# Running states of a recurrence carried as two chains of two head pairs, with operands stored chunk by chunk

## The chip, the cores and the metric

The kernel runs on one core of a Trainium2 chip. The metric is device time in microseconds (us). The engines are TensorE (PE; PEld is its weight load), VectorE (DVE), ScalarE (ACT), GpSimd (POOL) and the queue engine SyncE (SP), which issues nearly all DMAs here in program order.

## The reference, cut to what matters

The reference is two transformer blocks over 1,024 tokens of 1,024 features. The first block normalises x, multiplies by `w_in`, and feeds two branches: latent attention (MLA, eight heads) and a recurrence (RWKV, eight heads of 64 channels, in both directions of time).

```python
h = rms_norm(x, norm_mix_g[l])
z = h @ w_in[l]
o_mla = mla_branch(z_mla, ...)
o_rwkv = rwkv_branch(z_rwkv, ...)
gates = jax.nn.sigmoid(z_gate + gate_b[l])
mixed = gates[:, :, 0] * (o_mla @ w_br_mla[l]) + gates[:, :, 1] * (o_rwkv @ w_br_rwkv[l])
x = x + mixed @ w_out[l]
```

The rest (a hierarchical mixture of experts, then a block with windowed attention, a gated linear recurrence and expert-choice mixtures) doesn't touch the change. In the RWKV branch each head carries a 64 x 64 state over time. The kernel works in chunks of 64 tokens: all that needs no state is prepared for every chunk, and then the state is carried over 16 chunks, in each direction.

## The kernel before, in words

Tokens are T = 1024, chunks CH = 64, so NCH = 16. A *head pair* puts two heads on 128 partitions; there are four pairs, and each has two directions d.

`phase_a` computes 37 column tiles of z one after the other (`z_tile`: 48 products of 128x512 each) and calls `after(m)` behind each. In `after`, tiles 5, 8, 11 and 14 complete a pair's inputs. `pair(j)` then runs `prep` for the four combinations of half g and direction d, and behind the first of them `inverse(j - 1)` and `rwkv_chain` of pair j - 1. At tile 16 come pair 3, `inverse(3)`, `finish(0, 0)`, the release of preparation's pools (`own.close()`), the chain of pair 3 in pools opened after that (`ch3` and `pc3`), and `finish` of pairs 1 to 3. `mla` comes last in the program, and `branch_out` behind it.

The tile framework places the instructions of each engine by a simulation of its own: what is issued earlier in the program has priority, and what is ready fills the gaps. So tiles of z and MLA's work, which come late in the program, stand between the steps of the recurrence on PE, VectorE and ScalarE. Each engine then works through its fixed order.

`prep` (line 601 on) writes nine parts of 64 columns per chunk to scratch memory `P.rw[p]`, of shape [8, 128, 2, 1152]: two chunks next to each other, [chunk pair, partition, direction, part and chunk]. `put` (L489) stores a tile of eight chunks; `flip` (L525 to L535) transposes a tile and stores it in two DMAs. `inverse` solves a triangular system for each chunk of a pair by a long row of small VectorE instructions (L653, L655), joins the blocks by products (L671, L676), and stores X^T of four units (direction, half), written at L679.

`rwkv_chain` (L717 on) holds one pair in both directions. Per chunk it makes four groups of 64x64x64 products at L732, each into the one PSUM tile `pc` and each evicted before the next: p1 (L739, L740), U (the same lines), the new state S (L773, with the decayed old state SW that POOL makes at L755) and y (L777). VectorE takes partitions 0 to 63 of p1 and U, ScalarE the others. Every second chunk one load of 1,152 KB brings the operands of two chunks (L745), and y of two chunks is stored by two DMAs (L780). The tiles SW, p1, U and S have two buffers.

`finish(p, g)` (L682 on) sums y of both directions, normalises it per head (first product at L688), adds a bonus and a gate and stores half of the pair's output (L2006). It needs all chunks of its pair.

`branch_out` (L983 on) multiplies both branches by their output weights (tiles br).

Of the kernel before, what the change touches and what calls it, by code (L numbers as in the profile page):

```python
# [7 lines left out]
F32 = mybir.dt.float32  # L8
# [19 lines left out]
# ---------------------------------------------------------------- host layout  # L28

def _cols(w, idx):  # L30
    """[K, M] -> [len(idx)//128, 128, (K//128)*128]: tile, k-partition, (k-block, column)."""
    K = w.shape[0]
    t = w[:, idx].reshape(K // 128, 128, len(idx) // 128, 128)
    return np.ascontiguousarray(t.transpose(2, 1, 0, 3).reshape(len(idx) // 128, 128, K))


def _fvec(v):
    """[n*128] -> [128, n]: feature on the partition."""
# [3 lines left out]
def _chunks(w):  # L42
    """[..., K, N] -> [..., N/512 * K/512, 128, 2048]: chunks of 4 k-blocks by 512 columns, k fastest."""
# [7 lines left out]
def _constants():  # L51
    """Constants of the branches, and those of the whole program."""
# [138 lines left out]
# ---------------------------------------------------------------- device program  # L191

class Prog:
# [3 lines left out]
    def consts(self, pool, temp):  # L197
        """pool: for the whole program; temp: for the branches."""
# [17 lines left out]
    def keep(self, keep, dram):  # L216
        """Scratch memory, and the small tiles that several phases use."""
        nc = self.nc
        self.kp = keep
        self.yd = [dram.tile([128, T], F32, name=f"yd{j}") for j in range(8)]  # L220
# [3 lines left out]
        self.rw = [dram.tile([8, 128, 2, 1152], F32, name=f"rw{p}") for p in range(4)]  # L224
# [30 lines left out]
    def slots(self, table, n, base):  # L255
        """What marks the rows in table [128, 8, n, 6]: the row of its block plus base, the block and zero."""
# [5 lines left out]
    def thirds(self, table, x):  # L262
        """x in three bfloat16 parts that add up to it exactly, to table[..., 3:6]; x is overwritten."""
# [7 lines left out]
    def iota8(self, pool):  # L271
        """The slots (from 1), each eight times."""
# [4 lines left out]
    def onehot(self, out, iota8, pm):  # L277
        """out [128, 128, 8]: 1 at the slot pm (from 1) of each row and row block, 0 elsewhere."""
        return self.nc.vector.tensor_tensor(out, iota8, pm[:, None, :].to_broadcast([128, 128, 8]), op=OP.is_equal)

    def mm3(self, ps, lh, ll, rh, rl, first, last):
        """One K block of a float32 product from operands split into float32r parts."""
# [5 lines left out]
    def order(self, later, first):  # L288
        """`later` is issued behind `first` on their engine: one accumulation at a time in a bank."""
# [3 lines left out]
    def rsqrt(self, pool, out, v, n):  # L293
        """out = v ** -0.5 by Newton steps; out, v: [128, n]."""
# [16 lines left out]
    def rsqrt1(self, pool, out, v):  # L311
        """The same for one column where ScalarE has its square root at hand."""
# [9 lines left out]
def s1(P, hpool, wpool, psum):  # L322
    """Reads x, normalises it and leaves its transpose, split, in hT (hi, lo)."""
# [1711 lines left out]
```

## Time and profile before

| what | value |
|---|---|
| runs of the kernel before | 4,285.96, 4,307.15, 4,308.72 us; median 4,307.15 |
| span of the profiled execution | 4,303.5 us |
| PE busy | 3,854.9 us (90%) |
| PEld busy | 3,100.3 us (72%) |
| VectorE busy | 2,887.8 us (67%) |
| ScalarE busy | 2,145.3 us (50%) |
| POOL busy | 418.9 us (10%) |
| DMA | 925 MB, mean 215 GB/s |

The profile is of one execution. Busy time is the union of an engine's instructions; a matmul's end is modelled, so a busy PE isn't a PE at its peak. Idle time before an instruction is put down to what ended last. "Issue" is time in which an engine waited for nothing that the profile shows. Times in the rows below are microseconds from the span's start, durations of single instructions nanoseconds where a row says mean ns or min/median/max.

### The profile page before, as it was taken

Reading aid. Unit: us, or ns where it says so; the run is one execution under the profiler, and the core shown is the slowest. Engines: PE = TensorE matmul, PEld = TensorE weight load, DVE = VectorE, ACT = ScalarE, POOL = GpSimd, SP = SyncE. Lnnn points to the kernel's source line nnn. Section 1 sums busy time; section 2 is a strip of 40 time slices with the busy share of each in tenths; the row PEclk is TensorE's granted clock in tenths of the full one; section 3 lists DMA queues with packets and bytes.
Section 4 is the critical chain, followed back from the end, with each engine's and each line's share of the span. In section 5 each row is a group of like instructions: output and inputs, shape, how many; then the busy total and the mean of one; then the engine's idle time right before and its main releaser. Section 6 shows DMA issues by size and latency. Waiting matters only on the chain. (4 is left out here: it accounts for less than half of the span.)

```text
span 4303.5 us, 57981 instructions
## 1 busy us (share of the span) xinstructions
PE 3854.9 (90%) x22154; PEld 3100.3 (72%) x22154; DVE 2887.8 (67%) x4690; ACT 2145.3 (50%) x2829; POOL 418.9 (10%) x328
## 2 busy tenths in 40 slices
PE   7999988898998897999799969999969986999994
PEld 6877766776876676665679857787748875788773
DVE  4556375858557546654446758888876776788887
ACT  4322223333243224555335536777756852677774
POOL 0000000000010003333000001111010000111101
PEclk9999988988899898999899979999979997999997
DMA  3455665453435557997332359999941155899994
GB/s 106 140 169 148 182 196 161 120 153 92 150 107 173 212 193 269 317 304 227 120 132 82 131 205 338 370 376 384 373 158 69 69 202 207 304 359 377 384 373 168
DMA packets 362342, 925.00 MB, mean 215 GB/s; under 512 B 147600, under 2 KB 205712, under 8 KB 290128
## 3 DMA queue, kind: packets, MB, share of 16 engines
q1 hardware_dynamic: 343632, 870.93, 56.4%
q0 software_dynamic: 18432, 50.36, 4.7%
q8 instruction: 175, 2.87, 0.3%
q14 instruction: 103, 0.84, 0.1%
HBM read 770.68 MB, written 167.25 MB: 218 GB/s over the span
## 5 line engine op out<-in xcount | busy, mean ns | idle before, releaser
L253 DVE TENSOR_TENSOR wlo<-wraw,whi 128x2048 fp32r<-128x2048 f32 x498 | 1134.2, 2289 | 307.1 <-ACT whi L253 303.8
L253 ACT ACTIVATE whi<-wraw 128x2048 fp32r<-128x2048 f32 x498 | 955.0, 1919 | 378.3 <-PE g L286 254.0
L285 PE MATMUL g<-wlo,xth 128*128 128x512 f32 x1280 | 510.0, 398 | 6.7 <-DVE wlo L253 6.7
L284 PE MATMUL g<-whi,xth 128*128 128x512 f32 x1280 | 513.7, 402 | 2.3 <-ACT xth L253 1.6
L286 PE MATMUL g<-whi,xtl 128*128 128x512 f32 x1280 | 508.4, 397 | 7.7 <-DVE xtl L253 7.3
L286 PEld LDWEIGHTS g<-whi,xtl 128*128 128x128 f32 x1280 | 243.5, 190 | 63.7 <-DVE xtl L253 12.7
L285 PEld LDWEIGHTS g<-wlo,xth 128*128 128x128 f32 x1280 | 244.0, 191 | 61.4 <-DVE wlo L253 9.1
L284 PEld LDWEIGHTS g<-whi,xth 128*128 128x128 f32 x1280 | 244.4, 191 | 57.3 <-ACT xth L253 3.9
L284 PE MATMUL z<-hT_hi,w_hi 128*128 128x512 f32 x592 | 243.0, 411 | 9.7 <-ACT w_hi L253 6.7
L1635 POOL DMA_INDIRECT e_xg<-xm,e_ix x32 | 75.5, 2359 | 1719.5 <-DVE e_ix L1633 956.6
L285 PE MATMUL z<-hT_lo,w_hi 128*128 128x512 f32 x592 | 242.0, 409 | 0.0
L286 PE MATMUL z<-hT_hi,w_lo 128*128 128x512 f32 x592 | 241.0, 408 | 0.0
L285 PE MATMUL g<-wlo,e_hh 128*128 128x512 f32 x512 | 202.4, 398 | 15.5 <-DVE wlo L253 15.5
L284 PE MATMUL g<-whi,e_hh 128*128 128x512 f32 x512 | 204.3, 400 | 8.2 <-ACT e_hh L253 8.0
L286 PE MATMUL g<-whi,e_hl 128*128 128x512 f32 x512 | 196.5, 391 | 0.2
L904 PE MATMUL po<-V,pts 128*128 128x64 f32 x1024 | 142.5, 285 | 6.3 <-DVE tab L856 4.9
L284 PEld LDWEIGHTS z<-hT_hi,w_hi 128*128 128x128 f32 x592 | 115.2, 195 | 41.5 <-ACT w_hi L253 7.4
L904 PEld LDWEIGHTS po<-V,pts 128*128 128x128 f32 x1024 | 135.4, 204 | 12.1 <-DVE tab L856 5.2
L755 POOL TENSOR_SCALAR SW<-S,wc 128x64 f32<-128x64 f32 x120 | 65.5, 563 | 785.0 <-DVE S L773 701.3
L285 PEld LDWEIGHTS z<-hT_lo,w_hi 128*128 128x128 f32 x592 | 115.0, 194 | 30.4 <-issue 4.5
L286 PEld LDWEIGHTS z<-hT_hi,w_lo 128*128 128x128 f32 x592 | 114.4, 193 | 30.0 <-issue 3.8
L1235 PE MATMUL g<-wraw,m_hT 128*128 128x512 f32 x256 | 120.3, 610 | 13.1 <-ACT m_y L1236 8.1
(531 smaller groups left out, 8308.7 us busy)
## 6 DMA issues: line engine op xcount, KB each, us to landing
wraw<-in_w_gu SPq DMA_DIRECT2D x256, 1024.0 KB
wraw<-in_w_dn SPq DMA_DIRECT2D x128, 1024.0 KB
wraw<-in_w SPq DMA_DIRECT2D x96, 1024.0 KB
rwt<-rw SPq DMA_DIRECT2D x32, 1152.0 KB
w_raw<-in_w_in SPq DMA_DIRECT2D x37, 512.0 KB
rw<-flip SPq DMA_DIRECT2D x96, 128.0 KB
rw<-rAR SPq DMA_DIRECT2D x16, 512.0 KB
gt<-z_out SPq DMA_DIRECT2D x16, 512.0 KB
```

The costliest lines, as they stand in the source:

```text
L253: return self.nc.scalar.activation(hi, src, AF.Copy), self.nc.vector.tensor_sub(lo, src, hi.bitcast(F32))
L284: t.matmul(ps, lh, rh, start=first, stop=False)
L285: t.matmul(ps, lh, rl, start=False, stop=False)
L286: t.matmul(ps, ll, rh, start=False, stop=last)
L755: nc.gpsimd.tensor_scalar(SW[:, d], S[:, d], P.wc[:, c, 4 * d + p:4 * d + p + 1], None, op0=OP.mult)
L904: i = nc.tensor.matmul(po[:, q], pt[:, k], V[:, 4 * q + k, 64 * par:64 * par + 64], start=(k == 0), stop=(k == 3))
L1235: nc.tensor.matmul(ps, ht[:, k], w[:, k, n], start=(k == 0), stop=(k == 1))
L1635: nc.gpsimd.indirect_dma_start(out=xg, out_offset=None, in_=self.x, in_offset=bass.IndirectOffsetOnAxis(ap=ix[:, :1], axis=0))
```

## The change

The running states are carried in two chains of two pairs each (q = 0: pairs 0 and 1; q = 1: pairs 2 and 3). In a chain the four combinations of pair and direction (u = 0 to 3) go through each chunk together: each group at L732 has twice the products, each eviction twice the columns (256). Chain 0 is issued behind `inverse(1)`, chain 1 behind `inverse(3)`, `finish(0, 0)` and `own.close()`, both with the pools `ch` and `pc`. `finish(1)` uses `pc3`.

The scratch memory becomes `P.rw[q]` of shape [16, 128, 2, 2, 576]: [chunk, partition, pair, direction, part], nine parts of 64 columns. Loads are one per chunk; stores write 64 columns (256 bytes) where they wrote 128; a flip is stored by four DMAs instead of two. y goes to `P.yd[q]` chunk by chunk in one DMA. SW, p1 and U have one buffer, S two. SW is one product of POOL with a broadcast instead of two scalings. The other lines of the diff take out comments and texts.

```diff
-        self.yd = [dram.tile([128, T], F32, name=f"yd{j}") for j in range(8)]
+        self.yd = [dram.tile([4, 128, T], F32, name=f"yd{j}") for j in range(2)]
...
-        self.rw = [dram.tile([8, 128, 2, 1152], F32, name=f"rw{p}") for p in range(4)]
+        self.rw = [dram.tile([NCH, 128, 2, 2, 576], F32, name=f"rw{p}") for p in range(2)]
...
     def put(self, p, d, g, m, t):
-        self.P.nc.sync.dma_start(self.P.rw[p][4 * g:4 * g + 4, :, d, 128 * m:128 * m + 128].rearrange("g p t -> p g t"),
-                                 t.rearrange("p (g c) t -> p g (c t)", c=2))
+        self.P.nc.sync.dma_start(self.P.rw[p // 2][NH * g:NH * g + NH, :, p % 2, d, CH * m:CH * m + CH]
+                                 .rearrange("c p t -> p c t"), t)
...
         for c in range(2):
-            o = 128 * m + 64 * c
-            nc.sync.dma_start(P.rw[p][4 * g:4 * g + 4, :, d, o:o + 64].rearrange("g (h t) k -> t (g h) k", h=2),
-                              t[64 * c:64 * c + 64].rearrange("t (x k) -> t x k", k=64))
+            x = t[64 * c:64 * c + 64].rearrange("t (g h k) -> t g h k", h=2, k=64)
+            for h in range(2):
+                nc.sync.dma_start(P.rw[p // 2][NH * g + c:NH * g + NH:2, 64 * h:64 * h + 64, p % 2, d,
+                                               CH * m:CH * m + CH].rearrange("g t k -> t g k"), x[:, :, h])
...
-        wc = P.wc[:, NH * g:NH * g + NH, 4 * d + p:4 * d + p + 1]
+        wc = P.wc[:, NH * g:NH * g + NH, 2 * p + d:2 * p + d + 1]
...
-        nc.sync.dma_start(P.rw[p][4 * g:4 * g + 4, :, d, 0:256].rearrange("g p t -> p g t"),
-                          AR.rearrange("p (g c) t -> p g (c t)", c=2))
+        nc.sync.dma_start(P.rw[p // 2][NH * g:NH * g + NH, :, p % 2, d, 0:128].rearrange("c p t -> p c t"), AR)
...
-        y, y1 = self.load("y0", P.yd[p], g), self.load("y1", P.yd[4 + p], 1 - g)
+        yd = P.yd[p // 2][2 * (p % 2):2 * (p % 2) + 2]
+        y, y1 = self.load("y0", yd[0], g), self.load("y1", yd[1], 1 - g)
...
-def rwkv_chain(P, pool, psum, p):
+def rwkv_chain(P, pool, psum, q):
...
-    U2 = range(2)
+    U4 = range(4)
...
-            for u in U2:
+            for u in U4:
...
     def ev(dst, ps):
-        nc.vector.tensor_copy(dst[0:64], ps[0:64, 0, 0:128].rearrange("p (u t) -> p u t", t=CH))
-        nc.scalar.activation(dst[64:128], ps[64:128, 1, 0:128].rearrange("p (u t) -> p u t", t=CH), AF.Copy)
+        nc.vector.tensor_copy(dst[0:64], ps[0:64, 0, 0:256].rearrange("p (u t) -> p u t", t=CH))
+        nc.scalar.activation(dst[64:128], ps[64:128, 1, 0:256].rearrange("p (u t) -> p u t", t=CH), AF.Copy)
 
     for c in range(NCH):
-        if c % 2 == 0:
-            R = pool.tile([128, 2, 1152], F32, name="rwt", bufs=2)
-            nc.sync.dma_start(R, P.rw[p][c // 2])
-            Y = pool.tile([128, 2, 2, CH], F32, name="Y", bufs=2)
-        o = c % 2
-        A, Rr = (R[:, :, 128 * o + CH * m:128 * o + CH * m + CH] for m in range(2))
-        LA, MB, MK, BT, KT, VT, XT = (R[:, :, 128 * m + CH * o:128 * m + CH * o + CH] for m in range(2, 9))
-        new = lambda name: pool.tile([128, 2, CH], F32, name=name, bufs=2)
+        R = pool.tile([128, 4, 576], F32, name="rwt", bufs=2)
+        nc.sync.dma_start(R, P.rw[q][c].rearrange("p a d t -> p (a d) t"))
+        Y = pool.tile([128, 4, CH], F32, name="Y", bufs=2)
+        A, Rr, LA, MB, MK, BT, KT, VT, XT = (R[:, :, CH * m:CH * m + CH] for m in range(9))
+        new = lambda name, bufs=1: pool.tile([128, 4, CH], F32, name=name, bufs=bufs)
         pst = lambda: psum.tile([128, 2, 512], F32, name="pc", bufs=1)
         if S is not None:
             SW = new("SW")
-            for d in U2:
-                nc.gpsimd.tensor_scalar(SW[:, d], S[:, d], P.wc[:, c, 4 * d + p:4 * d + p + 1], None, op0=OP.mult)
+            nc.gpsimd.tensor_tensor(SW, S, P.wc[:, c, 4 * q:4 * q + 4][:, :, None].to_broadcast([128, 4, CH]),
+                                    op=OP.mult)
...
-            Sn = new("S")
+            Sn = new("S", 2)
             for h in range(2):
-                src = ps[h2[h], h, 0:128].rearrange("p (u t) -> p u t", t=CH)
+                src = ps[h2[h], h, 0:256].rearrange("p (u t) -> p u t", t=CH)
...
-            nc.scalar.activation(Y[h2[h], :, o], ps[h2[h], h, 0:128].rearrange("p (u t) -> p u t", t=CH), AF.Copy)
-        if o:
-            for d in range(2):
-                nc.sync.dma_start(P.yd[4 * d + p][:, CH * (c - 1):CH * (c + 1)], Y[:, d].rearrange("p c t -> p (c t)"))
+            nc.scalar.activation(Y[h2[h]], ps[h2[h], h, 0:256].rearrange("p (u t) -> p u t", t=CH), AF.Copy)
+        nc.sync.dma_start(P.yd[q][:, :, CH * c:CH * c + CH].rearrange("u p t -> p u t"), Y)
...
-                rwkv_chain(P, p("ch3"), pc3, 3)
-                finish(1)
+                rwkv_chain(P, ch, pc, 1)
+                finish(1, pc3)
...
-                        rwkv_chain(P, ch, pc, j - 1)
+                        if j == 2:
+                            rwkv_chain(P, ch, pc, 0)
```

## Rows read from the trace of the kernel before

**Rows 1.** Windows by stage: length, engines' busy, granted clock, DMA share, GB/s.

```profile
590.00:700.00 110.00, 81.96 (x610) 65.18 (x609) 61.53 (x123) 27.21 (x61) 10.43 (x16) 0.71 0.57 168
700.00:1140.00 440.00, 395.13 (x3378) 324.02 (x3379) 300.62 (x741) 154.19 (x384) 29.79 (x56) 0.86 0.48 136
1140.00:1360.00 220.00, 216.90 (x2551) 175.03 (x2549) 142.00 (x406) 94.63 (x262) 22.19 (x49) 1.00 0.36 119
1360.00:1500.00 140.00, 107.65 (x510) 78.77 (x510) 86.08 (x156) 39.51 (x52) 2.01 (x4) 0.84 0.63 220
```

**Rows 2.** The same view for line L732 alone: PE and PEld busy.

```profile
430.00:590.00 160.00, 16.82 (x384) 13.33 (x384) 0.97 0.59 183
590.00:700.00 110.00, 17.46 (x328) 14.26 (x328) 0.71 0.57 168
...
sum 955.00, PE 176.53 PEld 144.49; mean PE 44.13 PEld 36.12
```

**Rows 3.** Groups by line, 430 to 1,390: busy us, mean ns; idle before, releasers.

```profile
L755 POOL TENSOR_SCALAR SW<-S,wc 128x64 f32<-128x64 f32 x120 | 65.5, 563 | 785.0 <-DVE S L773 701.3 <-DVE S L771 83.5
L894 DVE COPY pts<-pt 128x512 f32<-128x512 f32 x64 | 43.9, 686 | 10.9 <-PE pt L889 9.7 <-PE po L904 0.5
L777 ACT ACTIVATE Y<-pc 64x128 f32<-64x128 f32 x128 | 34.5, 269 | 78.4 <-PE pc L732 76.9
L773 DVE TENSOR_TENSOR S<-pc,SW 64x128 f32<-64x128 f32 x112 | 32.2, 288 | 33.8 <-PE pc L732 32.7
L739 DVE COPY p<-pc 64x128 f32<-64x128 f32 x64 | 17.8, 279 | 32.7 <-PE pc L732 32.4
```

**Rows 4.** Waits, 430 to 1,390: engine, line, releaser; us in total, times, longest.

```profile
PEld pc L732 <- issue: 46.6, 107, 2.1
PE pc L732 <- ACT U L740: 10.7, 7, 2.9
PE pc L732 <- DVE S L773: 9.2, 8, 2.0
```

**Rows 5.** Line L773 in two windows: min/median/max ns, first and last start.

```profile
L773 DVE TENSOR_TENSOR S<-pc,SW x28: 272/289/295, 808.2 to 1034.7; 64x128 f32<-64x128 f32 x28
L773 DVE TENSOR_TENSOR S<-pc,SW x28: 274/289/295, 1200.3 to 1276.9; 64x128 f32<-64x128 f32 x28
```

**Rows 6.** Inverse(3)'s outputs (line L679), and chain 0's start on the timeline.

```profile
L679 DVE TENSOR_TENSOR rXT<-pw,xt x4: 424/425/425, 1095.7 to 1131.2; 128x256 f32<-128x256 f32 x4
...
432.89 2.13 SPq L745 DMA_DIRECT2D rwt<-rw  x2
439.35 0.69 PE L732 MATMUL pc<-rwt 64*64 64x64 f32 x8
```

**Rows 7.** Timeline (start us, us) around the stage's end; attention's products; branch_out's products.

```profile
1370.36 1.13 PE L688 MATMUL pc<-y,cstb 128*128 128x512 f32 x2 [0.51 <-DVE yc L713]
1382.56 0.80 SPq L780 DMA_DIRECT2D yd<-Y  x2
1390.99 1.99 PE L688 MATMUL pc<-y,cstb 128*128 128x512 f32 x2
1421.39 1.02 PE L688 MATMUL pc<-y,cstb 128*128 128x512 f32 x2
1456.25 0.32 SPq L2006 DMA_DIRECT2D orw<-yc  x1
...
L904 PE MATMUL po<-V,pts x1024: 217/275/475, 706.9 to 1359.8; 128*128 128x64 f32 x171
...
L284 PE MATMUL br<-oh,whi x128: 387/392/1414, 1392.0 to 1581.5; 128*128 128x512 f32 x128
```

**Rows 8.** DMA from 160 to 1,140 (980 us), and the flips' issues (min/median/max ns).

```profile
DMA packets 204753, 150.57 MB, mean 154 GB/s; under 512 B 125369, under 2 KB 177337, under 8 KB 201867
q1 hardware_dynamic: 204675, 149.53, 52.3%
L534 SPq DMA_DIRECT2D rw<-flip x96: 574/627/1990, 199.7 to 1000.9; - x96
```

## Prediction

> **What bounds the kernel now.** I first cut the span by stage [rows 1]: the change touches only the projection and the two branches, which end near 1,500 us; what lies behind runs on other data and should only shift. In these stages TensorE (PE) is the fullest engine: 217 of 220 us from 1,140 to 1,360, 395 of 440 before that, 82 of 110 from 590 to 700 (at a granted clock of 0.71) and only 108 of 140 from 1,360 to 1,500. VectorE has 301 of 440 us, ScalarE about half of that. So PE is nearly full while latent attention is there to fill it, and it has holes in two places: from 590 to 700, between the projection and attention, and from 1,360, behind attention's last product.
>
> Next I asked what the running states cost. Their products (L732) hold PE for 177 us, of which only 17 and 17 us lie before 590 and 700 [rows 2]. Their 64x128 evictions take 0.27 to 0.29 us each [rows 3]. Then the waits: PE stands still in front of L732 for 10.7 us behind the eviction of U and 9.2 us behind S; its weight loads stand 46.6 us in 107 pieces for no instruction that the trace shows, which is mostly the change from a 128-row to a 64-row product [rows 4]. That is small. The states matter as a chain of latencies: each chunk is four products and four evictions in strict order over one PSUM tile, so the length of a step is what counts. With inverse and preparation beside it a step takes (1034.7 - 808.2) / 13 = 17.4 us; where two of the four chains run side by side (28 adds are 7 joint steps), (1276.9 - 1200.3 - 1.0) / 6 = 12.6 us, the 1.0 being the second chain's lag [rows 5].
>
> Last, who ends the stage. Chain 3 may open its pools only when preparation's memory is released; it stores its last output at 1,382.6. The last pair's finish then begins at 1,391.0 and 1,421.4 and stores its second half at 1,456.3, while the output projection of the branches begins at 1,392 [rows 7]. So latency of states and finish, not PE, ends this stage.
>
> **The change part by part.** *Steps.* 64 steps of one pair become 32 steps of two pairs. Products are the same in number and size, so PE's 177 us stay. Evictions become 64x256. Between 0.279 us at 128 columns and 0.686 us at 512 [rows 3] a straight line gives 0.279 + 128 x 0.407 / 384 = 0.41 us. VectorE: 64 x 4 x 0.28 = 72 us become 32 x 4 x 0.41 = 53; ScalarE about 69 become 50. These 19 us each lie beside PE and are worth nothing by themselves. POOL's 120 products of 64 columns (0.563 us) become 30 of 256 columns; between 0.56 and 4 x 0.563 = 2.25 us each, I take the middle, and either end is hidden, because SW is wanted only three evictions later.
>
> *The last chain.* It no longer waits for the pools behind `own.close()`, only for the first outputs of inverse(3). These come at 1,095.7 to 1,131.2, four of them evenly [rows 6]; chunk 0 needs the first two, 1,107.5. From a load's issue to its first product took 439.35 - 432.89 = 6.5 us [rows 6]; with the store ahead of it I take 8.5, so it starts at 1,116. For 16 joint steps the bounds are 12.6 and 17.4 us [rows 5]. The nearest row is the joint one, which has this very work; four steps still stand beside inverse and the first finish, so 12 x 12.6 + 4 x 17.4 = 221 us: end at 1,337 (1,318 to 1,394). The joint row pays two evictions per hop where one 64x256 will do: 2 x 0.279 - 0.41 = 0.15 us, four hops, 16 steps: 9 us less, 1,328.
>
> *The finish.* Where only pair 3 was left behind the last chain, pairs 2 and 3 are now: four halves. Pair 1 gets a PSUM tile of its own and leaves the tail. The first half began 8.4 us after the last store (1,382.6 to 1,391.0). Successive halves began 20.6 us apart (1,370.4 to 1,391.0) and 30.4 us apart where the output projection ran beside them, and the last half took 34.9 us from there to its store [rows 7]. I take 20.6 twice and the middle, 25.5, once: 1,328 + 8.4 + 66.7 + 34.9 = 1,438, against 1,456.3: 18 us gained (with the ends of the spacing 13 to 23; with the ends of the step 27 gained to 48 lost).
>
> *PE's own sum.* The 34 us of products before 700 [rows 2] move behind it, as the first chain now waits for inverse(1), and 17 of them were done in the thin stretch 590 to 700. Against it: half of the stalls, 19.9 / 2 = 10 us; of the 46.6 us in front of weight loads half would go if each were a change of product size, 23, and none if not: 12; and the projection ends up to 17 us earlier, of which attention, whose start needs VectorE and ScalarE too, can use between 0 and 17: 8. Attention's last product moves from 1,359.8 [rows 7] to 1,360 + 34 - 10 - 12 - 8 = 1,364 (at worst 1,394). Both are ahead of 1,438, so PE doesn't set the end, but only just.
>
> *Layout.* Stores of L, B and K parts, X^T and the masks (64 DMAs) become 256-byte pieces where they were 512, AR's 16 DMAs 512 where they were 1,024, y 256 where it was 512: 32,768 + 8,192 + 8,192 = 49,000 more packets. At most each costs what a mean packet cost: 52.3% of 980 us over 204,753 packets is 2.5 ns of all 16 engines [rows 8], 123 us in 1,200, and the share goes from about 0.5 to 0.6; bytes are the same, so the other end is zero. Nothing in the stage waits for bandwidth at 0.6, so I book nothing; without that cover a store of X^T lands some 1.3 us later, four times on the path. The flips' 96 DMAs (already 256-byte pieces) become 192 of half the size: their issue costs 0.627 us [rows 8], so SP spends 0 to 60 us more in 16 preparations, up to 4 us each. Behind them on SP stand the loads of the next preparation and of the chain. I take it that the store that inverse waits for isn't the one behind them and book nothing, with 4 x 4 = 16 us at the far end. Loads of rwt stay 32 of 1,152 KB, but each now feeds one step and not two.
>
> The Trainium skill (DMA: Bandwidth & Descriptors, Specifications) speaks against this part: below 512 bytes a transfer falls under line rate, since the engine reads, modifies and writes. [...] The trace neither shows nor excludes it for these stores; its flips go to the same memory in 256-byte pieces already.
>
> *Buffers.* SW, p1 and U have one buffer where they had two. Each is overwritten only behind a product that precedes its writer on PE or VectorE anyway, so no wait is added. Sum: 4,303.5 - 18 = 4,285.5 us of span; the median of the runs, 4,307.15, stands 3.65 us above the span, so 4,289.
>
> **Rivals.** (1) *PE alone is the limit, and the tail closes.* If steps run faster than the joint row (VectorE has one eviction per hop and no second chain), the finishes slip under attention, and the output projection starts behind 1,364 and not at 1,392; with part of the 32 us of holes after 1,360 [rows 1] that is 28 to 40 us: about 4,273. For it: PE is idle 32 us there. Against it: joint steps still took 12.6 us with PE full. (2) *The step is late for its data.* One load per step with two buffers leaves one step, 12.6 us, from a buffer's release to its next use, and a load needs 6.5 us plus SP's delay; before, it had two steps. SP issues in order; if it is over 6 us late, each step grows to the 17.4 us row: the end is 1,394 instead of 1,337, 57 us, and so 39 us lost instead of 18 gained: about 4,346. For it: the load sits on a queue with many waiting stores. Against it: among PE's waits in front of L732 the longest are for evictions, none of these for a load [rows 4]. (3) *The moved work binds.* Attention ends at 1,394, the projection of the branches starts after it: 34 us late, less the 18 to 26 that the tail gives: about 4,317. For it: 590 to 700 gets emptier, and its clock of 0.71 would be no better. (4) *The small pieces cost more than booked.* Stores hold each of four preparations up by the 4 us of SP and the 1.3 us of the store: 21 us, about 4,310. For it: all of it lies ahead of the last chain. Against it: bytes are the same. The rule of the Trainium skill's DMA page named above would act here.
>
> **How the numbers follow.** Forecast 0.45 (4,289, own spread 20 either way), rival 1 0.22, rival 2 0.15, rival 3 0.12, rival 4 0.06. Half a per cent, 21.5 us, is about what a measurement of this kernel can tell from no change: below 4,286 is faster, above 4,329 slower. The forecast puts 0.20 below and 0.25 inside; rival 1 goes below, rivals 3 and 4 mostly inside, rival 2 above with some of 3 and 4: 0.42, 0.39, 0.19. The range runs from 4,248 (rival 1 with the forecast's best step) to 4,340.
>
> **What would show it.** Right: the last chain's first load at about 1,112, joint adds 12 to 13 us apart, its last output at 1,320 to 1,345, attention's last product by 1,375 and the last finish stored near 1,440. Adds 17 us apart with PE waiting for rwt show rival 2; attention ending past 1,385 rival 3; a last store of the finish before 1,400 rival 1; X^T of inverse(3) after 1,145 rival 4. The forecast is wrong altogether if the planned order around inverse moves, so that its outputs come tens of microseconds elsewhere.

## The result, and the profile after

The changed kernel took 4,322.75 us (median of 4 runs, 4,319.75 to 4,332.88) against 4,304.61 (4 runs, 4,285.96 to 4,308.72): a ratio of 1.0058, 95% interval [1.0039, 1.0078]. It is slower by 0.6%, where 4,289 was forecast. The profiled execution spans 4,331.1 us, 27.6 more than the kernel before. It is the slowest of the four runs (4,332.88), 10 us above their median, so the times below hold some 10 us that aren't the change's; one trace can't tell where they lie.

First the windows by stage (length, busy time of PE, PEld, VectorE, ScalarE and POOL, granted clock, DMA share, GB/s), which answer to [rows 1]:

```profile
440.00:590.00 150.00, 140.53 (x665) 111.46 (x664) 72.54 (x162) 40.46 (x62) 0.00 (x0) 0.93 0.59 171
590.00:700.00 110.00, 80.79 (x416) 62.88 (x417) 69.62 (x143) 31.30 (x64) 2.71 (x6) 0.70 0.46 121
700.00:1140.00 440.00, 389.70 (x3779) 322.75 (x3777) 307.76 (x703) 151.32 (x347) 16.37 (x25) 0.88 0.53 142
1140.00:1360.00 220.00, 205.48 (x2545) 168.00 (x2546) 129.42 (x332) 80.37 (x193) 8.95 (x13) 0.96 0.44 146
1360.00:1500.00 140.00, 98.51 (x563) 67.56 (x562) 70.12 (x145) 26.79 (x36) 1.23 (x2) 0.69 0.51 178
```

PE has more holes than before in every one of them (from 440 to 590 it was busy all 150 us), and most in the stage that [rows 1] showed nearly full: 14.5 us of 220 free from 1,140 to 1,360, where it was 3. PE became less full while the time grew, so the added time isn't added work of PE. The next view is of the single lines that end the stage: the third pair's inverse (L679), the last chain's adds of S (L772) and stores of y (L777), the finish's first product (L689) and its stores (L2004). Columns are min/median/max ns, then the first and last start; the window is 1,055 to 1,500, where L2004 stores all eight halves and L689 works on pairs 1 to 3, twice per half.

```profile
L679 DVE TENSOR_TENSOR rXT<-pw,xt x4: 425/425/425, 1111.8 to 1143.1; 128x256 f32<-128x256 f32 x4
...
L772 DVE TENSOR_TENSOR S<-pc,SW x28: 405/422/428, 1173.6 to 1381.1; 64x256 f32<-64x256 f32 x28
...
L777 SPq DMA_DIRECT2D yd<-Y x16: 370/371/624, 1156.5 to 1394.8; - x16
...
L2004 SPq DMA_DIRECT2D orw<-yc x8: 319/320/320, 1162.9 to 1487.9; - x8
...
L689 PE MATMUL pc<-y,cstb x12: 590/1059/1221, 1186.6 to 1454.4; 128*128 128x512 f32 x12
```

The inverse's first output comes 16 us later than in [rows 6], its last 12. The chain's steps are (1394.8 - 1156.5) / 15 = 15.9 us apart, neither 12.6 nor 17.4 [rows 5]. The last y is stored 12 us later than before and the last half of the finish at 1,487.9, 31.6 us later [rows 7]. What follows that store is the same: 4,303.5 - 1,456.3 = 2,847 us before, 4,331.1 - 1,487.9 = 2,843 after. So the whole loss of this execution has been made when that store is issued.

The single instructions cost what was expected. Groups from 430 to 1,400 us (busy us, mean ns; idle before):

```profile
L776 ACT ACTIVATE Y<-pc 64x256 f32<-64x256 f32 x64 | 24.2, 377 | 51.9 <-PE pc L734 51.4
L772 DVE TENSOR_TENSOR S<-pc,SW 64x256 f32<-64x256 f32 x56 | 23.6, 421 | 15.6 <-PE pc L734 15.1
L753 POOL TENSOR_TENSOR SW<-S,wc 128x256 f32<-128x256 f32 x30 | 22.2, 741 | 547.3 <-DVE S L772 487.2 <-DVE S L770 60.0
L741 DVE COPY p<-pc 64x256 f32<-64x256 f32 x32 | 13.2, 413 | 15.8 <-PE pc L734 15.5
```

The 64x256 eviction takes 0.41 us, as the straight line through [rows 3] gave. What makes a step long is seen on the timeline of one (start us, us; PE's products and the evictions, weight loads and POOL left out):

```profile
1272.97 0.86 DVE L772 TENSOR_TENSOR S<-pc,SW 64x256 f32<-64x256 f32 x2 [0.21 <-PE pc L734]
...
1274.96 0.68 PE L734 MATMUL pc<-rwt,S 64*64 64x64 f32 x16
...
1275.48 0.63 PE L734 MATMUL pc<-rwt 64*64 64x64 f32 x16
...
1275.94 0.63 PE L734 MATMUL pc<-rwt,U 64*64 64x64 f32 x16
1276.62 0.77 ACT L776 ACTIVATE Y<-pc 64x256 f32<-64x256 f32 x2
...
1277.93 0.68 PE L734 MATMUL pc<-S,rwt 64*64 64x64 f32 x16
...
1278.45 0.63 PE L734 MATMUL pc<-rwt 64*64 64x64 f32 x16
1279.13 0.42 DVE L741 COPY p<-pc 64x256 f32<-64x256 f32 x1
1280.39 0.38 ACT L742 ACTIVATE p<-pc 64x256 f32<-64x256 f32 x1
...
1282.61 0.68 PE L734 MATMUL pc<-p,rwt 64*64 64x64 f32 x16
1283.34 0.42 DVE L741 COPY U<-pc 64x256 f32<-64x256 f32 x1 [0.37 <-PE pc L734]
1283.79 0.38 ACT L742 ACTIVATE U<-pc 64x256 f32<-64x256 f32 x1 [0.15 <-DVE U L741]
...
1286.12 0.68 PE L734 MATMUL pc<-rwt 64*64 64x64 f32 x16
```

Four groups stand one behind the other: y, p1, U, S. None begins before the group ahead of it has been evicted from the one tile `pc`, and after each eviction 0.5 to 2 us pass until PE's order comes back to the chain (1277.39 to 1277.93, 1280.77 to 1282.61, 1284.17 to 1286.12). PE isn't idle in the pauses, it is in attention's products (busy all 100 us from 1,240 to 1,340); but with both pairs in step there is no second chain whose products could stand there.

Two more looks at the same chain. In the stretch in which attention fills PE and no half of the finish stands beside the chain, the steps are (1340.1 - 1244.9) / 6 = 15.9 us, so the finish beside the first steps isn't what makes them long:

```profile
L777 SPq DMA_DIRECT2D yd<-Y x7: 370/371/377, 1244.9 to 1340.1; - x7
```

Behind attention a step took 10.5 us (stores at 1,340.1 and 1,350.6), and then two took 17.4 and 18.0. In the first of these ScalarE stood 6.4 us for a load of attention's output, with the eviction of U behind it in its order; in the second PE had products of the branches' output projection between the groups. Against the step before them these two cost 14 us more.

```profile
1358.53 0.63 ACT L253 ACTIVATE oh<-oraw 128x512 fp32r<-128x512 f32 x1 [6.39 <-DMA oraw<-om]
1359.18 0.38 ACT L742 ACTIVATE U<-pc 64x256 f32<-64x256 f32 x1
```

DMA from 160 to 1,140 us, and then the flips' issues (min/median/max ns), which answer to [rows 8]:

```profile
DMA packets 249181, 145.84 MB, mean 149 GB/s; under 512 B 199248, under 2 KB 222160, under 8 KB 246800
## 3 DMA queue, kind: packets, MB, share of 16 engines
q1 hardware_dynamic: 249104, 144.82, 53.4%
```

```profile
L535 SPq DMA_DIRECT2D rw<-flip x192: 574/615/1922, 201.3 to 1037.5; - x192
```

44,428 more packets raised the share by 1.1 points; those under 512 bytes rose by 73,879, since stores of 512 bytes became pairs of 256. Per byte the engines were held 5% longer (53.4 / 144.82 against 52.3 / 149.53).

### The profile page after: what moved, and what is told of

Read it like the earlier page. It is cut to its first block, busy times and chain, and to the rows that moved or that the text cites. A ratio compares the mean times of both kernels' runs of the same rounds, so it can differ in the third digit from the quotient of the medians.

```text
span 4331.1 us, 57644 instructions
## 1 busy us (share of the span) xinstructions
PE 3845.1 (89%) x22154; PEld 3095.0 (71%) x22154; DVE 2881.3 (67%) x4566; ACT 2129.2 (49%) x2701; POOL 374.0 (9%) x238
## 5 line engine op out<-in xcount | busy, mean ns | idle before, releaser
L284 PE MATMUL z<-hT_hi,w_hi 128*128 128x512 f32 x592 | 243.0, 410 | 10.5 <-ACT w_hi L253 7.9
L880 ACT ACTIVATE p<-S,nm 128x512 f32<-128x512 f32 x128 | 87.4, 685 | 124.3 <-DVE nm L878 111.4
L1232 PE MATMUL g<-wraw,m_hT 128*128 128x512 f32 x256 | 119.5, 606 | 12.6 <-ACT m_y L1233 6.3
```

Source lines behind the costliest of these rows:

```text
L284: t.matmul(ps, lh, rh, start=first, stop=False)
L880: nc.scalar.activation(p, S, AF.Exp, bias=nm, scale=sc, accum_out=rs[:, b, q:q + 1])
L1232: nc.tensor.matmul(ps, ht[:, k], w[:, k, n], start=(k == 0), stop=(k == 1))
```

## The experiments

All ratios are to the kernel before on the same chip, with 95% intervals. Because every kernel spends 2,839 to 2,849 us behind the last store of the finish, the table of four times from the traces tells nearly all of each profiled execution. One execution of each kernel was traced, and the runs of one kernel lie 4 to 35 us apart, so a difference of a few microseconds between two rows says nothing. "X^T" is the first output of the third pair's inverse (pairs counted from 0), "last y" and "last half" are the last stores of the last chain and of the finish.

| kernel | ratio | X^T | last y | last half | span |
|---|---|---|---|---|---|
| before | 1 | 1,095.7 | 1,382.9 | 1,456.3 | 4,303.5 |
| the change | 1.0058 | 1,111.8 | 1,394.8 | 1,487.9 | 4,331.1 |
| e1_layout | 0.9942 | 1,074.0 | 1,371.5 | 1,440.2 | 4,288.6 |
| e3_first_joint | 1.0001 | 1,110.8 | 1,387.3 | 1,452.0 | 4,295.9 |
| e4_last_joint | 0.9983 | 1,070.5 | 1,356.0 | 1,451.0 | 4,294.1 |
| e5_two_psum | 1.0030 | 1,110.7 | 1,349.6 | 1,481.7 | 4,325.2 |
| e6_free_finish | 1.0037 | 1,101.2 | 1,385.4 | 1,471.9 | 4,317.9 |
| e7_flips_four | 0.9972 | 1,073.2 | 1,358.9 | 1,441.6 | 4,282.2 |
| e8_tail_one_pair | 0.9985 | 1,109.2 | 1,397.9 | 1,456.3 | 4,302.0 |
| e9_no_chain0 | 0.9950 | 1,091.0 | 1,359.4 | 1,423.1 | 4,262.4 |
| e10_two_tiles_early | 0.9938 | 1,086.0 | 1,295.4 | 1,433.3 | 4,279.6 |
| e11_two_tiles_pair1_first | 0.9971 | 1,087.4 | 1,364.9 | 1,455.6 | 4,295.4 |
| e12_loads_swapped | 0.9932 | 1,061.8 | 1,356.0 | 1,422.0 | 4,267.8 |
| e13_one_memset | 0.9991 | 1,087.9 | 1,375.6 | 1,448.7 | 4,298.1 |
| e14_after_swapped | 1.0015 | 1,096.3 | 1,371.5 | 1,463.6 | 4,309.6 |
| e15_after_memset | 1.0053 | 1,109.1 | 1,388.7 | 1,481.8 | 4,322.8 |
| e16_layout_swapped | 0.9989 | 1,103.9 | 1,380.2 | 1,461.0 | 4,301.0 |
| e17_two_tiles_swapped | 0.9986 | 1,100.0 | 1,312.3 | 1,453.3 | 4,292.6 |

**The parts alone.** The stores, the first joint chain and the last one can be taken apart: `rwkv_chain1` is the loop of before for one pair, reading the new layout with one load of two chunks; where a kernel also has a joint chain, it has that one's buffers. (The joint chains on the old layout weren't tried.)

e1_layout, the stores alone:

```diff
-                        if j == 2:
-                            rwkv_chain(P, ch, pc, 0)
+                        rwkv_chain1(P, ch, pc, j - 1)
...
-                rwkv_chain(P, ch, pc, 1)
-                finish(1, pc3)
+                rwkv_chain1(P, p("ch3"), pc3, 3)
+                finish(1)
```

> The layout of the change alone: scratch memory chunk by chunk, 64-column stores and four DMAs per flip, but four chains of one pair as before (one load of two chunks). Theory 1, the tail (one long last chain with four finish halves behind it costs the time): within 8 us of the kernel before, inverse(3)'s outputs within 5 us of 1,096 to 1,131. Theory 2, the layout (small stores and the doubled flips delay preparation): 12 to 25 us slower than before, inverse(3)'s outputs at about 1,112 to 1,143 as in the kernel after.

Measured: 4,278.85 us, ratio 0.9942 [0.9918, 0.9966]. The new stores don't slow this kernel; whether they speed it up is taken up again below.

e3_first_joint, the stores and the first joint chain, then pairs 2 and 3 alone:

```diff
+                        if j == 3:
+                            rwkv_chain1(P, ch, pc, 2)
...
-                rwkv_chain(P, ch, pc, 1)
-                finish(1, pc3)
+                rwkv_chain1(P, p("ch3"), pc3, 3)
+                finish(1)
```

> Layout of the change and a joint first chain (pairs 0 and 1), but pairs 2 and 3 as two chains of one pair in the places of before. Theory 1: the tail is that of before, so within 8 us of the kernel before, last state output near 1,385. Theory 2: 12 to 25 us slower than before. If the joint first chain itself cost time, it would be slower than the layout alone.

Measured: 4,299.36 us, ratio 1.0001 [0.9983, 1.0019]. Against e1 the third inverse's outputs come 37 us later, the last y 16 and the last half 12.

e4_last_joint, the stores and the last joint chain:

```diff
-                        if j == 2:
-                            rwkv_chain(P, ch, pc, 0)
+                        if j < 3:
+                            rwkv_chain1(P, ch, pc, j - 1)
```

> The stores of the change, pairs 0 and 1 in chains of one pair as before, pairs 2 and 3 in the joint last chain. Theory A (each part has a price of its own: stores -0.6%, first chain +0.6%, last chain +0.6%): steps of the last chain 15 to 17 us apart, its last y store near 1,385, the last store of the finishes 88 to 93 us behind that, near 1,475; ratio to the kernel before 0.999 to 1.004. Theory B (the joint last chain only costs what the joint first chain makes late): the last chain starts near 1,085 instead of 1,126, the last store of the finishes is at 1,445 or before, ratio 0.995 or less.

```profile
L772 DVE TENSOR_TENSOR S<-pc,SW x28: 405/422/429, 1131.7 to 1334.8; 64x256 f32<-64x256 f32 x28
...
L777 SPq DMA_DIRECT2D yd<-Y x16: 370/371/732, 1115.2 to 1356.0; - x16
```

Measured: 4,291.73 us, ratio 0.9983 [0.9971, 0.9995], between the two theories. The steps are 16.1 us as in the change, and the tail from the last y to the last half is 95.0 us; but the inverse's outputs are back at 1,070.5, so the long steps and the long tail belong to the last joint chain. The late inverse goes with the first one in the kernels so far; how far that holds is taken up again below.

**The tail.** e6_free_finish and e8_tail_one_pair let finishes behind the last chain read the y of pairs that are long done, and leave out their own y (e6 for pairs 2 and 3, e8 for pair 2):

```diff
 e6_free_finish
-        yd = P.yd[p // 2][2 * (p % 2):2 * (p % 2) + 2]
+        yd = P.yd[0][2 * (p % 2):2 * (p % 2) + 2]
 e8_tail_one_pair
+        yd = P.yd[p // 3][2 * (p % 2):2 * (p % 2) + 2]
...
-                finish(2)
-                finish(3, pc3)
+                finish(2, pc3)
+                finish(3)
```

> The kernel after, but the finishes of pairs 2 and 3 read y of pairs 0 and 1, so that they needn't wait for the last chain (y of pairs 2 and 3 isn't used). Theory 1: the four halves go under the last chain; the branches' output starts when attention ends and the stage ends with it: 50 to 90 us below the kernel after, 4,235 to 4,275. Theory 2: preparation's delay stays, 0 to 35 us below the kernel after.

Measured: 4,319.51 us, ratio 1.0037 [1.0018, 1.0056]. The finishes still began at 1,385 to 1,438, although their y had long been there: pair 2 is finished on `pc`, which the chain holds to its end (its first product, at 1,385.4, had waited for the last eviction of y), and pair 3 behind pair 2. This run priced nothing; the next one gave pair 2 the other tile.

> The change, but the finish of pair 2 reads the y of pair 0 and has the PSUM tile of pair 1's finish, so that only pair 3 is finished behind the last chain. Left out: pair 2's own y is not used. If the tail's two added halves are what the joint last chain costs, the last store comes 65 to 75 us behind the last y store (88 to 93 with the change), near 1,465, and the ratio falls from 1.006 to 0.999 to 1.002. If the chain itself is what is late, the last store stays within 8 us of that of the change and the ratio is 1.004 or more.

```profile
L777 SPq DMA_DIRECT2D yd<-Y x16: 370/371/987, 1147.8 to 1397.9; - x16
L2004 SPq DMA_DIRECT2D orw<-yc x8: 319/320/383, 1154.2 to 1456.3; - x8
```

Measured: 4,294.98 us, ratio 0.9985 [0.9970, 1.0000]. The last y came as late as with the change, the last half 58.4 us behind it and not 93 (65 to 75 were expected). The two halves that the change adds behind its last chain are worth 1.0058 - 0.9985 = 0.7%, about the whole loss. That is what they cost, not what made the kernel slower: they were foreseen, and an earlier end of the chain was to pay for them.

**The step.** e5_two_psum gives the y products of the last chain a PSUM tile of their own:

```diff
-        ps = pst()
+        ps = pst(other or psum)
         mm(ps, lambda u: ([(S[:, u], Rr[:, u])] if S is not None else []) + [(VT[:, u], MK[:, u]), (Ut[:, u], MB[:, u])])
...
-                rwkv_chain(P, ch, pc, 1)
+                rwkv_chain(P, ch, pc, 1, pc3)
```

> The kernel after, but in the last chain the group for y has a PSUM tile of its own (that of pc3), so the next chunk's first group needn't wait for y's eviction. Theory 1: the step of the last chain falls from 15.9 us to 12 to 13.5, its last output from 1,395 to about 1,345 to 1,360, and the time 30 to 45 us below the kernel after, about 4,275 to 4,295. Theory 2: the start of the last chain is what counts, so 0 to 10 us below the kernel after.

Measured: 4,319.60 us, ratio 1.0030 [1.0003, 1.0057]. The y stores run from 1,185.8 to 1,349.6, 10.9 us apart, but they begin 29 us later, since `pc3` opens late, and pair 1's finish now waits for the same tile, so six halves stand behind the chain: the step of theory 1, without its time. e10_two_tiles_early removes the late start (on the base of e4, with pair 0's finish issued ahead of the third inverse), and e11_two_tiles_pair1_first also takes pair 1's finish out of the tail:

```diff
 e10_two_tiles_early
-                R.inverse(3)
                 finish(0, 0)
+                R.inverse(3)
                 own.close()
                 R.big, pc3 = p("fin"), p("pc3", space=PS)
-                rwkv_chain(P, ch, pc, 1)
+                rwkv_chain(P, ch, pc, 1, pc3)
                 finish(1, pc3)
 e11_two_tiles_pair1_first
+                finish(1)
                 rwkv_chain(P, ch, pc, 1, pc3)
-                finish(1, pc3)
```

> Pairs 0 and 1 in chains of one pair, the last chain joint, with its y products in a PSUM tile of their own (pc3), which opens sooner because the finish of pair 0 is issued ahead of the third inverse. Theory S (the step is long because all four groups go through one PSUM tile): the last chain's y stores come 11 to 13 us apart from the start (16.1 with one tile), it ends at 1,290 to 1,320 instead of 1,356; six halves of the finish follow, 17 to 19 us apart, and the last store comes at 1,415 to 1,450, ratio 0.992 to 0.998. Theory C (the short steps seen with two tiles came from a start after the inverse and the first finish): steps stay at 15 to 17 us, the end at 1,350 or later, and with six halves behind it the last store near 1,480, ratio over 1.003.

The same lines of this kernel, and a piece of one step:

```profile
L772 DVE TENSOR_TENSOR S<-pc,SW x28: 416/423/428, 1124.4 to 1282.4; 64x256 f32<-64x256 f32 x28
...
L777 SPq DMA_DIRECT2D yd<-Y x16: 359/371/385, 1114.3 to 1295.4; - x16
...
L2071 SPq DMA_DIRECT2D orw<-yc x7: 319/320/457, 1074.7 to 1433.3; - x7
```

```profile
1203.39 0.68 PE L734 MATMUL pc<-rwt 64*64 64x64 f32 x16
1203.90 0.63 PE L734 MATMUL pc<-U,rwt 64*64 64x64 f32 x16
1204.37 0.63 PE L734 MATMUL pc<-rwt,U 64*64 64x64 f32 x14
1204.65 0.86 DVE L772 TENSOR_TENSOR S<-pc,SW 64x256 f32<-64x256 f32 x2 [2.25 <-PE pc L734]
1205.04 0.77 ACT L776 ACTIVATE Y<-pc 64x256 f32<-64x256 f32 x2 [3.95 <-PE pc L734]
```

Measured: 4,280.35 us, ratio 0.9938 [0.9921, 0.9955], with steps of 12.1 us from the start. The products of y (pc<-rwt,U) follow those of S at once, and both are evicted side by side: three pauses per step, not four. The chain ends at 1,295.4, and even six halves behind it leave the last one at 1,433.3. PE was as full beside this chain (177 of 180 us from 1,115 to 1,295) as beside the change's (176 of 180 from 1,160 to 1,340), so the step beside attention is long because of its one tile: 12.1 us against 15.9.

> As the run with two PSUM tiles and an early start, but pair 1 is finished ahead of the joint last chain, on its tile, so that only four halves are left behind it. Theory S: steps of 11 to 13 us, but the chain starts only when that finish has left the tile, at 1,140 to 1,190; end at 1,330 to 1,375, last store 88 to 95 us later at 1,420 to 1,470, ratio 0.993 to 1.001. Theory C: steps of 15 us or more, last store at 1,480 or later, ratio over 1.003.

Measured: 4,292.69 us, ratio 0.9971 [0.9953, 0.9989]: steps of 12.3 us, but a first y at 1,180, since the chain waits for pair 1's finish to leave `pc`; last half at 1,455.6, 91 us behind the last y. Against e10 the tail is 47 us shorter, but the chain ends 69 us later: the later start took more than the shorter tail gave.

**The stores once more.** e7_flips_four is the kernel before with nothing but four DMAs per flip:

```diff
+            x = t[64 * c:64 * c + 64].rearrange("t (g h k) -> t g h k", h=2, k=64)
+            for h in range(2):
+                nc.sync.dma_start(P.rw[p][4 * g:4 * g + 4, 64 * h:64 * h + 64, d, o:o + 64].rearrange("g t k -> t g k"),
+                                  x[:, :, h])
```

> The kernel before, with each transposed tile stored by four DMAs instead of two; shapes in memory and all else as before. If the gain of the stores (ratio 0.994 with all of them) comes from the flips being cut in four, the outputs of the third pair's inverse come near 1,075 instead of 1,096 and the ratio is 0.993 to 0.997. If it comes from the rest of the stores or from another planned order, the outputs stay near 1,096 or move by under 10 us and the ratio is 0.998 to 1.003. If the 53 us of issue time on SP that they add hurt, the outputs come after 1,100 and the ratio is over 1.003.

Measured: 4,286.32 us, ratio 0.9972 [0.9955, 0.9988], X^T at 1,073.2. These are nearly the numbers of the theory that credits the flips. But any edit also lets the planner place the whole recurrence in another order. Two kernels with the work of before and another planned order test that:

```diff
 e12_loads_swapped
-        k = self.load("k", P.zr[3 * p + 1], tg)
         kn = self.load("nkk", P.kn[p], tg)
+        k = self.load("k", P.zr[3 * p + 1], tg)
 e13_one_memset
-        nc.vector.memset(self.ones, 1.0)
+        nc.vector.memset(self.ones, 1.0); nc.vector.memset(self.ones[:, 0:1], 1.0)
```

> The kernel before with two loads of preparation, k and nkk, issued in the other order: no work added or removed, but the planned order of the engines around the recurrence is another. Theory P (a few tenths of a per cent come from the planned order alone): outputs of the third inverse move by 5 us or more from 1,096 to 1,131, and the ratio differs from 1 by 0.002 or more, either way. Theory F (the gain of flips cut in four is the stores' own): outputs stay within 5 us and the ratio within 0.002.

```profile
L679 DVE TENSOR_TENSOR rXT<-pw,xt x4: 423/424/426, 1061.8 to 1097.6; 128x256 f32<-128x256 f32 x4
...
L2006 SPq DMA_DIRECT2D orw<-yc x8: 319/320/772, 1119.1 to 1422.0; - x8
```

Measured: 4,269.94 us, ratio 0.9932 [0.9901, 0.9964]. Two loads in the other order brought the inverse's outputs 34 us forward and gave the lowest ratio of all.

> The kernel before with one more memset of a single column at the start, work of under 0.1 us: the planned order of the engines is another from there on. Theory P: outputs of the third inverse move by 5 us or more, and the ratio differs from 1 by 0.002 or more, either way. Theory F: outputs stay within 5 us and the ratio within 0.002.

```profile
L679 DVE TENSOR_TENSOR rXT<-pw,xt x4: 424/424/424, 1087.9 to 1123.3; 128x256 f32<-128x256 f32 x4
...
L2006 SPq DMA_DIRECT2D orw<-yc x8: 319/320/320, 1143.2 to 1448.7; - x8
```

Measured: 4,300.12 us, ratio 0.9991 [0.9976, 1.0006]: outputs 8 us earlier, time the same. So the planned order alone can be worth 0 to 0.7%, as much as all that was to be explained. (The swap is no gain in itself: below, it made two other kernels 0.5% slower.) The same two edits were therefore laid over the change and over two of the variants.

> The change with the two loads k and nkk of preparation issued in the other order, which alone made the kernel before 0.7% faster by another planned order. Theory T (the loss is the change's own: longer steps through one PSUM tile and four halves of the finish behind them): steps of the last chain stay at 15 to 17 us, the tail at 85 to 95 us, and against the kernel before with the same swap (0.993) it is 0.4 to 1.2% slower, a ratio of 0.997 to 1.005 to the kernel before. Theory O (the loss was an unlucky planned order): ratio under 0.996.

Measured: 4,308.02 us, ratio 1.0015 [1.0002, 1.0027]; steps of 15.4 us, tail 92.1.

> The change with one more memset of a column at the start, which gives another planned order and left the kernel before at 0.999. Theory T: third inverse's first output at 1,100 to 1,115, steps 15 to 17 us, tail 85 to 95 us, ratio 1.002 to 1.008. Theory O: ratio under 0.999.

Measured: 4,322.98 us, ratio 1.0053 [1.0033, 1.0073]; steps of 15.9 us, tail 93.1.

```profile
L679 DVE TENSOR_TENSOR rXT<-pw,xt x4: 417/424/425, 1109.1 to 1137.6; 128x256 f32<-128x256 f32 x4
...
L777 SPq DMA_DIRECT2D yd<-Y x16: 370/371/750, 1150.8 to 1388.7; - x16
L2004 SPq DMA_DIRECT2D orw<-yc x8: 319/319/320, 1157.2 to 1481.8; - x8
```

Edit for edit the change is slower each time: 1.0058 as it stands, 1.0015 / 0.9932 = 1.008 with the loads swapped, 1.0053 / 0.9991 = 1.006 with the memset. The memset moves little, so these are hardly more than two orders; in them the loss stays with the change.

> The stores of the change alone (four chains of one pair) with the two loads swapped. Against the kernel before with the same swap (0.993): if the stores bring a gain of their own of about 0.6%, the ratio is 0.985 to 0.989; if their 0.994 came from the planned order, it lies between 0.990 and 1.000, and the first output of the third inverse between 1,060 and 1,096 as in the other kernels with four chains.

Measured: 4,293.48 us, ratio 0.9989 [0.9974, 1.0003], X^T at 1,103.9, 8 us past the range named. With the same swap the kernel before has 0.9932, so here the stores look 0.6% slower, where e1 had them 0.6% faster. Neither need be theirs: the stores have no effect that can be told from the planned order, and the gain that e1 and e7 seemed to show isn't shown.

> Joint last chain with y in a PSUM tile of its own and an early start (0.994), with the two loads swapped. If what sets the end is the outputs of the third inverse plus a last chain of 16 steps of 12.1 us and six halves, the last store comes 330 to 350 us behind the first of these outputs (347 without the swap), whatever the planned order; ratio 0.986 to 0.998.

Measured: 4,294.59 us, ratio 0.9986 [0.9973, 1.0000]. The last half came 353 us behind the first X^T, a little over the 330 to 350 expected, with steps of 11.4 us. The short step holds in another order; the gain of e10 over the kernel before does not. Here the inverse came 14 us later than in e10, and against the kernel before with the same swap (0.9932) this one is 0.5% slower.

**The first joint chain.** e9_no_chain0 is e1 without the chain of pair 0, whose finish reads the y of pair 1:

```diff
-                        rwkv_chain1(P, ch, pc, j - 1)
+                        if j > 1:
+                            rwkv_chain1(P, ch, pc, j - 1)
```

> The stores of the change, chains of one pair as before, but pair 0's chain is left out (its finish reads the y of pair 1). Nothing of the recurrence's states runs before about 640 us, as with the joint first chain, but there is no more work later either. Theory D (the joint first chain costs what its work displaces in the 700 to 1,030 us stretch, where inverses and preparation want VectorE): outputs of the third pair's inverse come at 1,075 or before, as with the stores alone, and the last store of the finishes at 1,440 or before, ratio 0.994 or less. Theory G (the cost is the gap itself: another planned order of preparation once nothing of the chain stands in 440 to 640): outputs come at 1,100 or later, ratio 0.998 or more.

Measured: 4,279.11 us, ratio 0.9950 [0.9934, 0.9966], X^T at 1,091.0: between the two theories, and now known to be within what a planned order does. One thing it does show: a whole chain less, some 177 / 4 = 44 us of products [rows 2], isn't faster than e1 with all four (0.9942). So the first chain's price where it stood before is too small to be told from the planned order, and moving it can't have gained much.

## Why the prediction was wrong, step by step

**What bounds the kernel: right.** The end of the finish sets the end of the stage, and PE's amount of work doesn't. In all 18 kernels 2,839 to 2,849 us follow the last half.

**The third inverse's outputs: wrong.** The prediction took them from [rows 6] and moved the first chain without moving them; it named this only as what would upset it altogether. They came at 1,111.8 to 1,143.1. Over the planned orders tried, the first output lies at 1,096 to 1,112 in the seven kernels with a joint first chain (mean 1,107) and at 1,062 to 1,104 in the ten others with pair 0's chain by itself (mean 1,084): 23 us, though the groups overlap and several kernels of the first share most of their order. Between the kernel before and the change, in the three orders, the difference is 16, 35 and 21 us. Whether this comes from the chain's work that now lies beside inverse and preparation, or from the gap it leaves ahead of its first product at 683, the runs didn't settle.

**The step: the term that failed.** "The nearest row is the joint one, which has this very work": 12 x 12.6 + 4 x 17.4. The work is the same, the place isn't. In [rows 5] two chains run on two PSUM tiles, and each stands in the other's pauses. And the rest of PE's work stands in the pauses that are left. The row to start from was the lone chain of one pair, which the trace before has at its end:

```profile
L773 DVE TENSOR_TENSOR S<-pc,SW x14: 276/288/295, 1289.9 to 1368.5; 64x128 f32<-64x128 f32 x14
```

These are six intervals of (1368.5 - 1289.9 - 0.3) / 6 = 13.0 us, the 0.3 being the second half of the last add. Worked out afterwards, as an estimate: in step, a second pair adds its products to the path, 176.5 / 64 = 2.8 us [rows 2], and four evictions that are 0.13 us longer: 13.0 + 2.8 + 0.5 = 16.3 us, where the six kernels with the joint last chain on one tile show 15.4 to 16.7. From the first y to the last, 15 steps, the change took 238 us; predicted were 12 x 12.6 + 3 x 17.4 less 8 for the evictions, 195, so 43 us were missing. The runs with two tiles show the cause: 10.9 to 12.3 us, in four kernels. Some 10 of the 43 us (17.4 + 18.0 - 2 x 12.6) fell in the two steps behind attention, which the branches' work lengthened.

**The chain's start: right in kind, late.** It did start right behind the inverse and not behind `own.close()`. The first load went out at 1,125.8 and not at about 1,112, behind an X^T stored at 1,122.5: 14 us, the late inverse. From there to the first y's store 30.7 us passed beside the rest of the inverse, where 4 for the load and 17.4 for the step were taken: 9 us. Together 23 us, of which the step's part is again the term above.

**The finish: right in kind, too dear.** 8.4 + 66.7 + 34.9 = 110 us were booked behind the last y, 93.1 came: the spacing was 16 to 19 us instead of 20.6 to 25.5. So 1,438 + 23 + 43 - 17 = 1,487, and the profile shows the store at 1,487.9. The tail's 17 us hid a part of the other misses by luck; and some 10 us of the whole belong to this one execution.

**PE's own sum: wrong in its sign, without consequence.** Attention's last product came at 1,340.0, 20 us before that of the kernel before and not 4 us behind it (1,364): its first came at 644.8 and not at 706.9. In the tail PE waited, as predicted.

**Layout and buffers booked at nothing: not contradicted.** A 22% rise in packets raised the share from 52.3% [rows 8] to 53.4% where up to 123 us had been allowed, and SP's 96 added issues slowed neither e1 nor e7. A price of some 0.5% would be lost in the planned order: the stores look 0.6% faster in one, 0.6% slower in the other. No run shows the buffers alone. The Trainium skill's rule that below 512 bytes a transfer falls under line rate (DMA: Bandwidth & Descriptors, Specifications) agrees in direction with the 5% more engine time per byte; no run shows a price of it in the kernel's time.

**The rivals.** The forecast's gain of 18 us and rival 1 fell with the step. Rival 2 has its time nearest above, not its mechanism: from 430 to 1,400 us the largest group of the chain's products stood 0.4 us for rwt. Rival 3 has the nearest time, 4,317, but attention ended before 1,350. Rival 4's sign, X^T after 1,145, was nearly met (1,143.1), but e1 and e16 have the same stores and their last X^T at 1,110.1 and 1,136.4. What made the forecast wrong is in none of them: a longer step, from a serial path through one tile, beside a late inverse. Averaged over the three orders, the last half comes 35 us later, 24 of them by the inverse, for a cause that stays open, and 11 by a last stage that was to become 18 us shorter, for the long step.

## What to carry to other kernels

When two independent chains are put in step, price the step from a chain that runs alone, and add the second chain's products and evictions to its path; a row in which two chains overlap on two tiles already contains the gain that lockstep gives up. A group that nobody in the chain waits for (here y) belongs in another PSUM tile: it was worth 4 us of 16 in each step beside attention, at the price of the finishes that then wait for this tile. Where a planner lays out the order, run the unchanged work under one or two other orders before a difference of a few tenths of a per cent is put down to an edit.

## What the runs showed of the hardware

Stores cut to 256-byte pieces cost the DMA engines little: 204,753 packets [rows 8] and 249,181 for nearly the same bytes (150.57 and 145.84 MB) held the engines 52.3% and 53.4% of the time, 5% more per byte. One POOL product of 128x256 with a broadcast factor took 0.615 us in the middle (613 to 1,129 ns in the last chain, 0.741 us on the mean of both), 1.4 times the 0.443 us that a 128x64 scaling of the kernel before took in the middle, for four times the columns (on the mean 0.563 us [rows 3]). In the tail, with PE busy 98.5 of 140 us, the granted clock was 0.69 of full speed from 1,360 to 1,500, against 0.84 before, and the finish's 128x512 products, 0.59 us at the least (L689), took 1.03 to 1.22 us each there. So the serial tail ran its own few products slower, too.
